# A two-layer diffusion-transformer block on one core: the Exp table load moved to the start of the first scores, pooling bands of 136 columns, and even amounts of other work between layer 2's softmax units

## Chip, core and metric

The kernel runs on one core of a Trainium2 chip. The metric is the device time in microseconds. Each engine (PE for matmuls, DVE and ACT and POOL for the elementwise work, SP for issuing loads) carries out its own list of instructions in order; semaphores make an instruction wait for one of another engine. A difference of 0.2% (3.4 us here) is about what a measurement of this kernel can tell from no change.

## The reference

Two layers of a transformer with 256 image tokens and 256 context tokens, all in float32, batch 1, width 1024. Per layer:

```python
h_x = _half_ffn(h_x, ...); h_c = _half_ffn(h_c, ...)
a_x = _modulate(_rmsnorm(h_x, ...)); p_x = a_x @ w_in[l]
o_a = _neighbourhood_attn(q_a, k_a, v_a, k_a_c, v_a_c, na_rpb[l])   # 4 heads
o_b = _pool_mix(p_x[..., OFF_B_U:OFF_C_Q], pool_w[l], pool_scale[l]) # 4 groups of 64
o_c = _gqa_blocks(q_c, k_all, v_all)                                 # 8 query, 2 key heads
h_x = h_x + mod_x[:, :, 5] * (concatenate([o_a, o_b, o_c]) @ w_out[l])
h_x = _half_ffn(h_x, ...)
```

`_pool_mix` takes, for each of four groups of 64 channels, the mean over a window of 2, 4, 8 or 16 tokens less the token itself, and then a 64x64 product. In layer 1 (of the two) the context tokens go through attention and the second FFN as well; in layer 2 they only give keys and values. The factors `mod` come from `silu(c) @ w_ada`, 38 MB of weights for each layer, which are streamed in.

## The kernel before, in words

Weights come in over SP's queue as float32 blocks of 1 MB (three buffers, `raw`). ACT casts a half of a block to a high part (L309), DVE subtracts to get a low part (L312), and PE does three products for each pair (high-high, high-low, low-high: L351 to L353 in `mm3`). The order of the instructions is fixed when the program is written: `tick` advances a model clock by the estimated time of PE's work, and what was put off with `later` is written out when its time has come. On the chip only the order is left.

The attention part of a layer (`attention`) first makes the keys, the queries and the values of the neighbourhood part. Then `run` goes through the softmax units. Layer 2 has twelve, here u0 to u11; each is two heads for 128 queries: four matmuls for the scores (L1012, L1013), for each head the row maximum on DVE (L1029, with the bias addition L1028 for the first four units), the Exp on ACT (L1037, which also sums), the normalization on DVE (L1040, L1042), and, two units later (`DEPTH`), four transposes on PE for each head (`flip`, L1056) and the copy of the result to SBUF on ACT (L1064). When a pair of heads is complete, `pv` multiplies by the values (L1086) and splits the result (L1090, L1091). Units u4 to u11 need rotated queries, whose split in high and low parts (L892, L893) is `queries`.

Between scores and transposes stands other work for PE, so that the softmax has time: `fill(us)` takes pieces until the model clock has moved on by `us`. The amounts are in the table `FILL`: two numbers for each step of `run`, one list for each layer. The pieces, in this order: the rest of the input products (`rest_in`: four chunks of queries, each evacuated by ACT at L1148 and L1150 and followed by a small matmul for its statistics, L1155; then the values `u` of the pooling), one `pv` that is ready, the pooling (`pooled`), and then the output products of the first 512 inputs (`rest_out`, 96 matmuls in layer 2) in turn with quarters of an `ada` product (`run_ada`, L181, 8 in layer 2, each of which needs a block of 1 MB that has landed). After two chunks `q_post` rotates the queries (L903 on PE, L906 and L910 on DVE, L907 on POOL) and turns the statistics into factors (L392 and on). At the third unit the split of the other part's keys is written (`KEYS_AT`, L881 on ACT, L884 on DVE).

The scores and all these products share five PSUM banks (`mm`), the transposes two (`aux`): a product that is to begin in a bank waits until ACT or DVE has read what was in it.

`pooled` multiplies `u` by a banded matrix of 256x256 for each group. The diagonal blocks of 128x128 come from the tile `pmd` and two corners of 128x8 from `edge`, so that a group takes four matmuls (L1185 to L1187).

ACT's functions come in tables. The Exp table is loaded (ACT_TABLE_LOAD, at L1037) right in front of the first Exp of a layer's attention, and the Silu table again in the next FFN.

Of the kernel before, what the change touches and what calls it, by code (L numbers as in the profile page):

```python
# [9 lines left out]
F32 = mybir.dt.float32  # L10
F32R = mybir.dt.float32r
I32 = mybir.dt.int32
AF = mybir.ActivationFunctionType
# [22 lines left out]
ADA_TOT = (22.0, 22.0, 22.0, 22.0)  # L36
T2K = 12
DEPTH = (2, 2)
FILL = ((3.3, 2.6, 1.8, 2.6, 3.3, 5.5, 0, 0.6, 3.3, 0, 0.6, 1.2, 1.8, 0.6, 4.2, 2.6, 2.6, 0, 0, 0.6, 4.2, 0.6, 1.2, 0, 2.6, 1.2, 0, 1.8, 2.6, 1.2, 2.6, 0, 0.6, 1.2, 0.6, 0.6, 0, 0, 5.5, 2.6), (3.3, 0.6, 2.6, 3.3, 0.6, 3.3, 5.5, 0, 1.8, 1.8, 0.6, 1.8, 0.6, 5.5, 0, 1.2, 1.2, 1.2, 1.2, 1.2, 4.2, 1.2, 0.6, 0.6, 1.8, 0, 2.6, 0.6))
PACE = (0.8, 0.8, 0.8, 0.8, 0.7, 0.8)  # L40
AFTER = ((1.4, 3.5), (1.4, 3.5), (1.4, 3.5), (0.9, 3.0), (1.4, 3.5), (0.9, 4.1))
REFILL = (10.0, 13.0, 13.0, 4.5, 4.5)
# [8 lines left out]
def dit_kernel(  # L51
# [2 lines left out]
    x, c, ctx_in, c_ctx, w_ada, b_ada, norm_g,  # L54
    ffn1_up, ffn1_down, ffn2_up, ffn2_down, w_in, w_out,
    na_rpb, pool_w, pool_scale, q_norm_g, k_norm_g, final_g,
    k_ident, k_rot, k_rope, k_mask, k_pool, k_edge,
    out,
):
    nc = tc.nc  # L60
# [1 line left out]
    const = ctx.enter_context(tc.tile_pool(name="const", bufs=1))  # L62
# [23 lines left out]
    gsc = const.tile([128, 6, KD, 2], F32, name="gsc")  # L86
    hgt = const.tile([128, 4, KD, 2], F32, name="hgt")
    bm = const.tile([128, 2048], F32, name="bm")
    edge = const.tile([128, 2, 4, 8], F32, name="edge")
    pwbd = const.tile([128, 2, 128], F32, name="pwbd")  # L90

    def mm_bank(dt=F32):
# [711 lines left out]
    def attn_prep(l):  # L804

        if l == 0:
            ACT.dma_start(out=mask, in_=k_mask)
            ACT.dma_start(out=rot, in_=k_rot)
            ACT.dma_start(out=edge, in_=k_edge)
            ACT.dma_start(out=rope, in_=k_rope.rearrange("s p t -> p s t"))  # L810
        POOL.memset(bm, NEG)
        POOL.memset(pwbd, 0.0)
        for g in range(4):
            p0 = 64 * (g % 2)
            SP.dma_start(out=pwbd[p0:p0 + 64, g // 2, p0:p0 + 64], in_=pool_w[l, g])


        tab = dramp.tile([4, 64, 465], F32, tag="tab", name="tab")
        SP.dma_start(out=tab, in_=bass.AP(tensor=na_rpb.tensor, offset=l * 4 * 465, ap=[[465, 4], [0, 64], [1, 465]]))

        def go():
            braw = rawp.tile([128, 2048], F32, tag="raw", name="braw")
            bv = braw.rearrange("p (t h k) -> p t h k", t=2, h=4)
            for r in range(4):
                for h in range(4):
                    src = bass.AP(tensor=tab.tensor, offset=tab.offset + h * 64 * 465 + (7 - r) * 31 + 15, ap=[[464, 64], [31, 4], [1, 64]])
                    POOL.dma_start(out=bv[64 * (r % 2):64 * (r % 2) + 64, r // 2, h, :].rearrange("p (a b) -> p a b", a=4), in_=src)
# [14 lines left out]
    def attention(l, a, both):  # L842
# [8 lines left out]
        def carve(n, pat, **kw):  # L851
            r = B[:, o0[0]:o0[0] + n].rearrange(pat, **kw)
            o0[0] += n
            return r
# [3 lines left out]
        kc = carve(512, "p t -> p t")  # L858
        vc = carve(512, "p (b f) -> p b f", b=4)
        vcT = carve(512, "p t -> p t")  # L860
        A = a["t"]
        bmv = bm.rearrange("p (t h k) -> p t h k", t=2, h=4)
        O = [None]
# [113 lines left out]
            pass  # L977


        pmd = [tmp.tile([128, 512], F32, tag="t2k", bufs=T2K, name="pmd") for _ in range(2)]  # L980
        for b in range(2):
            ACT.dma_start(out=pmd[b].rearrange("p (g t) -> p g t", g=4), in_=k_pool[b])


        rq8 = small.tile([128, 40], F32, tag="rq8", bufs=1, name="rq8")
        PT = {}
# [11 lines left out]
        def scores(br, kind, hs, t):  # L998

            if kind == "gqa" and ("na", 0) in K:  # L1000
                for hp in range(2):
                    K.pop(("na", hp))
                st["out"] -= 2
                st["look"] = GQA_LOOK[l]
            S = [mm_bank() for _ in hs]
            q = queries(br, kind, hs)
            kt = K["na", hs[0] // 2] if kind == "na" else K["gqa"]
            keys = slice(0 if br == "x" else TX, NT)
            for tt in ((t,) if br == "x" else (0, 1)):
                for i in range(2):  # L1010
                    o = S[i] if br == "x" else S[i][:, tt * TX:(tt + 1) * TX]
                    PE.matmul(out=o, lhsT=q[:, i, tt * 128:(tt + 1) * 128], rhs=kt[:, i, keys], start=True, stop=False)  # L1012
                    PE.matmul(out=o, lhsT=q[:, i, tt * 128:(tt + 1) * 128], rhs=kt[:, 2 + i, keys], start=False, stop=True)  # L1013
            tick(0.9)
            return [soft(br, kind, h, t, S[i]) for i, h in enumerate(hs)]
# [161 lines left out]
        def pooled(v):  # L1177
            ps = mm_bank()
            pv_ = ps.rearrange("p (c t) -> p c t", c=2)
            for g in range(4):  # L1180
                r0 = 64 * (g % 2)
                o = pv_[r0:r0 + 64, g // 2, :]
                ug = [u[:, 2 * v + tb, g * 64:(g + 1) * 64] for tb in range(2)]
                for tb in range(2):
                    PE.matmul(out=o[:, tb * 128:(tb + 1) * 128], lhsT=ug[tb], rhs=pmd[tb][:, g * 128:(g + 1) * 128], start=(g < 2 and tb == 0), stop=False)  # L1185
                PE.matmul(out=o[:, 128:136], lhsT=ug[0], rhs=edge[:, 0, g, :], start=False, stop=False)
                PE.matmul(out=o[:, 120:128], lhsT=ug[1], rhs=edge[:, 1, g, :], start=False, stop=(g >= 2))  # L1187
            tick(1.7)
            y = tmp.tile([128, 512], F32, tag="t2k", bufs=T2K, name="y")
            ACT.copy(out=y, in_=ps)  # L1190

            def fin():
                ps2 = mm_bank()
                for ch in range(2):
                    PE.matmul(out=ps2[:, ch * TX:(ch + 1) * TX], lhsT=pwbd[:, ch, :], rhs=y[:, ch * TX:(ch + 1) * TX], start=True, stop=True)
                for ch in range(2):
                    s = colsB[:, 104 + 2 * l + ch:105 + 2 * l + ch]
                    oh, ol = acol(O[0], 2 + ch, v * TX, v * TX + TX)
                    ACT.activation(out=oh, in_=ps2[:, ch * TX:(ch + 1) * TX], func=AF.Copy, scale=s)
                    DVE.scalar_tensor_tensor(out=ol, in0=ps2[:, ch * TX:(ch + 1) * TX], scalar=s, in1=oh.bitcast(F32), op0=ALU.mult, op1=ALU.subtract)  # L1200
                missing[0] -= 1
            later(3.0, fin)
# [346 lines left out]
def _constants():  # L1549

    ident = np.eye(128, dtype=np.float32)
    rot = np.zeros((128, 128), np.float32)
    for f in range(128):
        i = f % 32
        if i < 16:
            rot[f + 16, f] = -1.0
        else:
            rot[f - 16, f] = 1.0
    pos = np.arange(256)
    inv = (np.float32(10000.0) ** (-np.arange(0, 32, 2, dtype=np.float32) / np.float32(32))).astype(np.float32)  # L1560
    ar = (pos // 64).astype(np.float32)[:, None] * inv[None]
    ac = (pos % 64).astype(np.float32)[:, None] * inv[None]
    head = np.concatenate([ar, ar, ac, ac], axis=1)
    ang = np.concatenate([head, head], axis=1).T
    rope = np.stack([np.cos(ang), np.sin(ang)]).astype(np.float32)
    col = np.arange(128) % 64
    kcol = np.arange(64)
    w0 = np.clip(col - 8, 0, 48)[:, None]
    mask = ((kcol[None] >= w0) & (kcol[None] < w0 + 16)).astype(np.uint32)
    pool = np.zeros((256, 4, 256), np.float32)  # L1570
    for g, w in enumerate((2, 4, 8, 16)):
        for t in range(256):
            lo, hi = max(t - w // 2, 0), min(t - w // 2 + w, 256)
            pool[lo:hi, g, t] = np.float32(1.0) / np.float32(hi - lo)
            pool[t, g, t] -= np.float32(1.0)
    blocks = np.stack([pool[0:128, :, 0:128], pool[128:256, :, 128:256]])
    edge = np.stack([pool[0:128, :, 128:136], pool[128:256, :, 120:128]], axis=1)
    return {"k_ident": ident, "k_rot": rot, "k_rope": rope, "k_mask": mask, "k_pool": np.ascontiguousarray(blocks), "k_edge": np.ascontiguousarray(edge)}


_INS = ['x', 'c', 'ctx', 'c_ctx', 'w_ada', 'b_ada', 'norm_g', 'ffn1_up', 'ffn1_down', 'ffn2_up', 'ffn2_down',
        'w_in', 'w_out', 'na_rpb', 'pool_w', 'pool_scale', 'q_norm_g', 'k_norm_g', 'final_g']
_CONST = ['k_ident', 'k_rot', 'k_rope', 'k_mask', 'k_pool', 'k_edge']
_OUTS = [((1, 256, 1024), 'float32')]


# [19 lines left out]
```

## Time and profile before

| what | value |
|---|---|
| median of 3 runs | 1686.69 us (1686.47 to 1686.74) |
| the profiled execution | 1686.64 us |
| its span, first to last instruction | 1684.9 us |
| PE busy | 1660.0 us (99%) |
| DVE, ACT, POOL busy | 1055.3, 663.8, 47.8 us |
| granted TensorE clock, mean | 0.998 |
| layer 1's softmax units | from 453.4 us |
| layer 2's softmax units | 1388.8 to about 1472.4 us |

The span is what the profile tells of; 1.7 us of the execution's time lie around it. In the timeline a row has a start, a duration, an engine, a line, an operation with its operands, a count when equal instructions were merged, and in brackets the idle time of the engine before it with what ended it. A matmul's row is longer than its place in the stream: the next one starts before it has drained.

### The profile page before, as it was taken

The page shows a single profiled execution, that of the slowest core. Times are in us where ns is not written, and L with a number is a line of the kernel's source. Part 1 is how long each engine was busy: PE and PEld are TensorE (multiplying, and loading weights), DVE is VectorE, ACT ScalarE, POOL GpSimd, SP SyncE. Part 2 cuts the span into 40 slices and gives each one's busy share as a digit, 9 for nine tenths or more (in the row PEclk, how much of TensorE's full clock was granted, in tenths as well). Part 3 has the DMA queues.
Part 4 walks back from the last instruction along what each step waited for, and adds up shares of the span by engine and source line. Part 5 has one row for each costly group of instructions (what it writes and reads, how often), then busy time and mean ns, then how long its engine had stood idle before and what let it go on. Part 6 is the DMA issues. An engine that isn't in the chain of part 4 may idle for free. (4 is left out here: it accounts for less than half of the span.)

```text
span 1684.9 us, 23252 instructions
## 1 busy us (share of the span) xinstructions
PE 1660.0 (99%) x9256; PEld 1401.6 (83%) x9256; DVE 1055.3 (63%) x1850; ACT 663.8 (39%) x1119; POOL 47.8 (3%) x67
## 2 busy tenths in 40 slices
PE   8999999999999999999999999999999999999997
PEld 5788888889896798888888898888888897799996
DVE  5676567667666776666764476545533567785665
ACT  4332323324556643223233243213232255664543
POOL 0000200000010000000000000020000000010000
PEclk9999999999999999999999999999999999999999
DMA  9755546531305425554553325564533223566551
GB/s 332 206 190 171 161 153 194 167 120 58 113 26 176 132 67 173 166 163 138 175 156 120 87 79 178 161 170 159 155 112 95 81 76 137 202 195 193 179 174 74
DMA packets 284932, 246.97 MB, mean 147 GB/s; under 512 B 9345, under 2 KB 249098, under 8 KB 282776
## 3 DMA queue, kind: packets, MB, share of 16 engines
q1 hardware_dynamic: 281992, 241.30, 46.2%
q0 software_dynamic: 1088, 2.15, 0.6%
q10 hardware_dynamic: 1744, 2.04, 0.4%
q8 instruction: 73, 1.20, 0.3%
q14 instruction: 35, 0.29, 0.1%
HBM read 244.40 MB, written 2.00 MB: 146 GB/s over the span
## 5 line engine op out<-in xcount | busy, mean ns | idle before, releaser
L351 PE MATMUL mm<-act,w 128*128 128x512 f32 (+1 forms) x2016 | 739.1, 367 | 0.0
L352 PE MATMUL mm<-act,w 128*128 128x512 f32 (+1 forms) x2016 | 733.0, 364 | 0.3 <-DVE act L435 0.3
L353 PE MATMUL mm<-act,w 128*128 128x512 f32 (+1 forms) x2016 | 732.9, 364 | 0.0
L312 DVE TENSOR_TENSOR w<-raw,w 128x1024 fp32r<-128x1024 f32 (+1 forms) x307 | 367.6, 1206 | 222.3 <-ACT w L309 221.9
L351 PEld LDWEIGHTS mm<-act,w 128*128 128x128 f32 x2016 | 380.5, 189 | 75.2 <-issue 14.1
L353 PEld LDWEIGHTS mm<-act,w 128*128 128x128 f32 x2016 | 380.4, 189 | 59.7
L352 PEld LDWEIGHTS mm<-act,w 128*128 128x128 f32 x2016 | 380.7, 189 | 59.1 <-DVE act L435 0.5
L309 ACT CAST w<-raw 128x1024 fp32r<-128x1024 f32 (+1 forms) x308 | 313.3, 1031 | 118.8 <-PE mm L353 96.9
L224 DVE SCALAR_TENSOR_TENSOR ada_acc<-ada_raw,sc,ada_acc 128x512 f32<-128x512 f32 x308 | 215.9, 747 | 37.9 <-DMA ada_raw<-in_w_ada_dram 20.9
L562 ACT CAST act<-gf 128x512 fp32r<-128x512 f32 x66 | 40.9, 620 | 269.9 <-DVE gf L559 269.9
L556 ACT ACTIVATE sil<-mm 128x512 f32<-128x512 f32 x66 | 39.3, 596 | 189.4 <-PE mm L353 184.5
L465 DVE SCALAR_TENSOR_TENSOR hT<-mm,hgt,hT 128x256 f32<-128x256 f32 x144 | 63.5, 480 | 76.9 <-PE mm L353 76.6
L559 DVE TENSOR_TENSOR gf<-sil,mm 128x512 f32<-128x512 f32 x65 | 44.7, 687 | 89.5 <-PE mm L353 75.7
L644 PE MATMUL mm<-act,w 128*128 128x258 f32 x352 | 100.2, 285 | 0.0
L645 PE MATMUL mm<-act,w 128*128 128x258 f32 x352 | 99.6, 283 | 0.0
L646 PE MATMUL mm<-act,w 128*128 128x258 f32 x352 | 99.5, 283 | 0.0
L563 DVE TENSOR_TENSOR act<-gf,act 128x512 fp32r<-128x512 f32 x66 | 45.7, 693 | 45.3 <-ACT act L562 45.3
L645 PEld LDWEIGHTS mm<-act,w 128*128 128x128 f32 x352 | 66.8, 190 | 0.3 <-DVE act L618 0.2
L644 PEld LDWEIGHTS mm<-act,w 128*128 128x128 f32 x352 | 66.6, 189 | 0.1
L646 PEld LDWEIGHTS mm<-act,w 128*128 128x128 f32 x352 | 66.4, 189 | 0.0
L377 ACT ACTIVATE sq<-hT 128x256 f32<-128x256 f32 (+1 forms) x45 | 22.5, 500 | 90.8 <-DVE hT L465 90.8
L441 ACT ACTIVATE act<-nt,modT 128x256 fp32r<-128x256 f32 x80 | 39.8, 508 | 37.8 <-DVE nt L440 37.8
(198 smaller groups left out, 1412.1 us busy)
## 6 DMA issues: line engine op xcount, KB each, us to landing
raw<-in_ffn_up_dram SPq DMA_DIRECT2D x170, 512.0 KB
ada_raw<-in_w_ada_dram SPq DMA_DIRECT2D x192, 256.0 KB
raw<-in_ffn_down_dram SPq DMA_DIRECT2D x35, 1024.0 KB
raw<-in_w_ada_dram SPq DMA_DIRECT2D x16, 1024.0 KB
raw<-in_w_in_dram SPq DMA_DIRECT2D x10, 1024.0 KB
raw<-in_ffn_down_dram SPq DMA_DIRECT2D x12, 768.0 KB
raw<-in_w_out_dram SPq DMA_DIRECT2D x8, 1024.0 KB
raw<-in_w_ada_dram SPq DMA_DIRECT2D x12, 512.0 KB
```

The costliest lines, as they stand in the source:

```text
L224: DVE.scalar_tensor_tensor(out=o, in0=raw, scalar=col, in1=o, op0=ALU.mult, op1=ALU.add)
L309: ACT.copy(out=wh, in_=sl)
L312: eng.tensor_tensor(out=wl, in0=sl, in1=wh.bitcast(F32), op=ALU.subtract)
L351: PE.matmul(out=ps, lhsT=wh, rhs=ah, start=start and i == 0, stop=False)
L352: PE.matmul(out=ps, lhsT=wh, rhs=al, start=False, stop=False)
L353: PE.matmul(out=ps, lhsT=wl, rhs=ah, start=False, stop=stop and i == last)
L465: DVE.scalar_tensor_tensor(out=hT[:, k, cols], in0=ps, scalar=gate[:, k, v:v + 1], in1=hT[:, k, cols], op0=ALU.mult, op1=ALU.add)
L559: DVE.tensor_tensor(out=u[:, 0:n], in0=s[:, 0:n], in1=pb[:, 0:n], op=ALU.mult)
L563: DVE.tensor_tensor(out=gl, in0=uv, in1=gh.bitcast(F32), op=ALU.subtract)
L644: PE.matmul(out=ps[:, 0:NX], lhsT=wh, rhs=ah, start=k == 0, stop=False)
L645: PE.matmul(out=ps[:, 0:NX], lhsT=wh, rhs=al, start=False, stop=False)
L646: PE.matmul(out=ps[:, 0:NX], lhsT=wl, rhs=ah, start=False, stop=k == KD - 1)
```

## The change

Three edits.

The Exp table: `scores` now writes, in each layer's first unit, one Exp of a single column (`ones` to `warm`) before the four matmuls, so that the table load stands in front of this one and no longer in front of the first real Exp.

The pooling: the two matrices become one, `bands`, of 136 columns for each half of the tokens, held in free columns of the tile `qkv`; a group takes two matmuls in place of four. The tile `edge` and its load go, and the two `pmd` tiles. The model time of `pooled` is 1.1 in place of 1.7.

The table: layer 2's 28 amounts (0 to 5.5, 48.9 in all) become 28 times 1.7 (47.6 in all). Layer 1's list stays.

```diff
-FILL = ((3.3, 2.6, ...), (3.3, 0.6, 2.6, 3.3, 0.6, 3.3, 5.5, 0, 1.8, 1.8, 0.6, 1.8, 0.6, 5.5, 0, 1.2, 1.2, 1.2, 1.2, 1.2, 4.2, 1.2, 0.6, 0.6, 1.8, 0, 2.6, 0.6))
+FILL = ((3.3, 2.6, ...), (1.7,) * 28)
...
-            ACT.dma_start(out=edge, in_=k_edge)
...
+        bands = carve(1088, "p (b g t) -> p b g t", b=2, g=4)
...
-        pmd = [tmp.tile([128, 512], F32, tag="t2k", bufs=T2K, name="pmd") for _ in range(2)]
         for b in range(2):
-            ACT.dma_start(out=pmd[b].rearrange("p (g t) -> p g t", g=4), in_=k_pool[b])
+            ACT.dma_start(out=bands[:, b], in_=k_pool[b])
...
             q = queries(br, kind, hs)
+            if not PT and not sums:
+
+                warm = small.tile([128, 8], F32, tag="nm", bufs=6, name="nm")
+                ACT.activation(out=warm[:, 0:1], in_=ones, func=AF.Exp)
...
                 ug = [u[:, 2 * v + tb, g * 64:(g + 1) * 64] for tb in range(2)]
-                for tb in range(2):
-                    PE.matmul(out=o[:, tb * 128:(tb + 1) * 128], lhsT=ug[tb], rhs=pmd[tb][:, g * 128:(g + 1) * 128], start=(g < 2 and tb == 0), stop=False)
-                PE.matmul(out=o[:, 128:136], lhsT=ug[0], rhs=edge[:, 0, g, :], start=False, stop=False)
-                PE.matmul(out=o[:, 120:128], lhsT=ug[1], rhs=edge[:, 1, g, :], start=False, stop=(g >= 2))
-            tick(1.7)
+                PE.matmul(out=o[:, 0:136], lhsT=ug[0], rhs=bands[:, 0, g], start=g < 2, stop=False, skip_group_check=True)
+                PE.matmul(out=o[:, 120:256], lhsT=ug[1], rhs=bands[:, 1, g], start=False, stop=g >= 2, skip_group_check=True)
+            tick(1.1)
```

What this does to the order shows best at three places of layer 2. The lines of the changed kernel are off by one or two from those of before (L910 is L909 there, L1029 is L1031, L1056 is L1058).

The first is ACT at the start of the softmax units, before and after. Exp is the ACTIVATE from `mm` to `P,sums`, two for each unit; the pairs that write `qkv` and `qsq` evacuate a chunk of queries; `K` is the split of keys. Before:

```order
L982 DMA pmd<-in_k_pool_dram 128x512 x2
L1037 ACT_TABLE_LOAD
L1037 ACTIVATE P,sums<-mm,nm 128x512 x2
L1148 ACTIVATE qkv<-mm,colsB 128x256
L1150 ACTIVATE qsq<-mm 128x256
L1037 ACTIVATE P,sums<-mm,nm 128x512 x2
L1148 ACTIVATE qkv<-mm,colsB 128x256
L1150 ACTIVATE qsq<-mm 128x256
L881 CAST K<-qkv 64x512 x4
```

The same place on ACT after the change, where L1008 is the new Exp of one column:

```order
L980 DMA qkv<-in_k_pool_dram 128x544 x2
L1008 ACT_TABLE_LOAD
L1008 ACTIVATE nm<-ones 128x1
L1039 ACTIVATE P,sums<-mm,nm 128x512 x4
L1150 ACTIVATE qkv<-mm,colsB 128x256
L1152 ACTIVATE qsq<-mm 128x256
L880 CAST K<-qkv 64x512 x4
L1039 ACTIVATE P,sums<-mm,nm 128x512 x2
L1150 ACTIVATE qkv<-mm,colsB 128x256
L1152 ACTIVATE qsq<-mm 128x256
```

The Exps of u0 and u1 now follow each other, and the second chunk of queries is evacuated behind the key split and the Exps of u2; it stood before the key split.

The second is DVE where the first two chunks of queries are rotated. `rot_t` is the product with the sines, the row that writes `qkv` from it finishes the rotation, and `rs_v` is the first step on the statistics, which reads them from their PSUM bank. Before:

```order
L1040 RECIPROCAL sums<-sums 128x1
L1042 TENSOR_SCALAR P<-P,sums 128x512
L906 TENSOR_TENSOR rot_t<-aux,rope 128x512
L910 TENSOR_TENSOR qkv<-qkv,rot_t 128x2x256
L392 TENSOR_SCALAR rs_v<-mm 128x8
```

The same two steps of the rotation on DVE after the change:

```order
L905 TENSOR_TENSOR rot_t<-aux,rope 128x512
L1030 TENSOR_TENSOR mm<-mm,bm 128x256
L1031 TENSOR_REDUCE nm<-mm 128x1
L1030 TENSOR_TENSOR mm<-mm,bm 128x256
L1031 TENSOR_REDUCE nm<-mm 128x1
L1042 RECIPROCAL sums<-sums 128x1
L1044 TENSOR_SCALAR P<-P,sums 128x512
L1042 RECIPROCAL sums<-sums 128x1
L1044 TENSOR_SCALAR P<-P,sums 128x512
L909 TENSOR_TENSOR qkv<-qkv,rot_t 128x2x256
L391 TENSOR_SCALAR rs_v<-mm 128x8
```

The maxima of u3 and the normalization of u2 now stand between the two steps of the rotation, and the statistics come after them.

The third is PE at the last units: `act,w` is `rest_out`, `ident,P` the transposes, `adasb` those of the ada rows, `PT` the products of values. Before, the last rows:

```order
L352 MATMUL mm<-act,w 128x256
L353 MATMUL mm<-act,w 128x256
L1056 MATMUL aux<-ident,P 128x128 x8
L249 MATMUL aux<-ident,adasb 128x128 x4
L1086 MATMUL mm<-PT,qkv 64x256 x16
```

The last rows of the softmax units on PE after the change, from the second head of u8 on:

```order
L1058 MATMUL aux<-ident,P 128x128 x4
L1014 MATMUL mm<-K,qst 128x512
L1015 MATMUL mm<-K,qst 128x512
L1014 MATMUL mm<-K,qst 128x512
L1015 MATMUL mm<-K,qst 128x512
L1058 MATMUL aux<-ident,P 128x128 x24
L1088 MATMUL mm<-PT,qkv 64x256 x16
```

Before, products of `rest_out` stand between the transposes of the last units; after, the transposes of u9, u10 and u11 (24) follow the last scores with nothing between, since the other work has been written out earlier.

More of the change, by code (lines that the diff above doesn't have):

```diff
@@ L38 @@
 DEPTH = (2, 2)
-FILL = ((3.3, 2.6, 1.8, 2.6, 3.3, 5.5, 0, 0.6, 3.3, 0, 0.6, 1.2, 1.8, 0.6, 4.2, 2.6, 2.6, 0, 0, 0.6, 4.2, 0.6, 1.2, 0, 2.6, 1.2, 0, 1.8, 2.6, 1.2, 2.6, 0, 0.6, 1.2, 0.6, 0.6, 0, 0, 5.5, 2.6), (3.3, 0.6, 2.6, 3.3, 0.6, 3.3, 5.5, 0, 1.8, 1.8, 0.6, 1.8, 0.6, 5.5, 0, 1.2, 1.2, 1.2, 1.2, 1.2, 4.2, 1.2, 0.6, 0.6, 1.8, 0, 2.6, 0.6))
+FILL = ((3.3, 2.6, 1.8, 2.6, 3.3, 5.5, 0, 0.6, 3.3, 0, 0.6, 1.2, 1.8, 0.6, 4.2, 2.6, 2.6, 0, 0, 0.6, 4.2, 0.6, 1.2, 0, 2.6, 1.2, 0, 1.8, 2.6, 1.2, 2.6, 0, 0.6, 1.2, 0.6, 0.6, 0, 0, 5.5, 2.6), (1.7,) * 28)
 PACE = (0.8, 0.8, 0.8, 0.8, 0.7, 0.8)
@@ L56, in dit_kernel @@
     na_rpb, pool_w, pool_scale, q_norm_g, k_norm_g, final_g,
-    k_ident, k_rot, k_rope, k_mask, k_pool, k_edge,
+    k_ident, k_rot, k_rope, k_mask, k_pool,
     out,
@@ L88, in dit_kernel @@
     bm = const.tile([128, 2048], F32, name="bm")
-    edge = const.tile([128, 2, 4, 8], F32, name="edge")
     pwbd = const.tile([128, 2, 128], F32, name="pwbd")
@@ L1575, in _constants @@
             pool[t, g, t] -= np.float32(1.0)
-    blocks = np.stack([pool[0:128, :, 0:128], pool[128:256, :, 128:256]])
-    edge = np.stack([pool[0:128, :, 128:136], pool[128:256, :, 120:128]], axis=1)
-    return {"k_ident": ident, "k_rot": rot, "k_rope": rope, "k_mask": mask, "k_pool": np.ascontiguousarray(blocks), "k_edge": np.ascontiguousarray(edge)}
+    bands = np.stack([pool[0:128, :, 0:136], pool[128:256, :, 120:256]])
+    return {"k_ident": ident, "k_rot": rot, "k_rope": rope, "k_mask": mask, "k_pool": np.ascontiguousarray(bands)}
 _INS = ['x', 'c', 'ctx', 'c_ctx', 'w_ada', 'b_ada', 'norm_g', 'ffn1_up', 'ffn1_down', 'ffn2_up', 'ffn2_down',
         'w_in', 'w_out', 'na_rpb', 'pool_w', 'pool_scale', 'q_norm_g', 'k_norm_g', 'final_g']
-_CONST = ['k_ident', 'k_rot', 'k_rope', 'k_mask', 'k_pool', 'k_edge']
+_CONST = ['k_ident', 'k_rot', 'k_rope', 'k_mask', 'k_pool']
 _OUTS = [((1, 256, 1024), 'float32')]
```

## Prediction

> **What bounds the kernel now.** I read the page first, then who PE waited for, then the timeline of layer 2's softmax units, engine by engine.
>
> ```profile
> PE 1660.0 (99%) x9256; PEld 1401.6 (83%) x9256; DVE 1055.3 (63%) x1850; ACT 663.8 (39%) x1119; POOL 47.8 (3%) x67
> ```
>
> PE is busy for all but 1% of the span, so the end is set by PE's work and by what it waits for. Its waits behind the start, with totals in us, are few:
>
> ```profile
> PE mm L1012 <- ACT P L1037: 1.3, 1, 1.3
> PE aux L1056 <- ACT PT L1064: 1.1, 1, 1.1
> PE ada L181 <- DMA raw<-in_w_ada_dram: 1.0, 1, 1.0
> ...
> PE mm L1155 <- DVE rs_v L392: 0.4, 1, 0.4
> ```
>
> These four are all in layer 2's softmax units, one each: the bank behind the first Exp, a copy of transposes, an ada block, the statistics' bank. With two more of 0.2, at the pooling (its row stands below) and at the last units, they make six and 4.2 us. Layer 1's units show none, so only layer 2 has anything to win. The stretch as a whole (busy us of PE, PEld, DVE, ACT, POOL):
>
> ```profile
> 1388.80:1472.40 83.60, 79.37 (x611) 62.12 (x609) 62.65 (x163) 53.22 (x112) 3.64 (x4) 1.00 0.48 166
> ```
>
> DVE is busy 62.65 of 83.6 us, ACT 53.22: both keep up on average, but three quarters busy and in order, so it matters where their work stands. The old table of amounts left six small waits; the question is how many the even one leaves.
>
> **The change, part by part.** PE's units of time, from the starts of scores (four matmuls, 1388.82 to 1389.75: 0.93) and of products (0.12 from start to start):
>
> ```profile
> 1388.82 0.40 PE L1012 MATMUL mm<-K,qst 128*128 128x512 f32 x1
> ...
> 1389.75 0.28 PE L351 MATMUL mm<-act,w 128*128 128x256 f32 x1
> 1389.87 0.28 PE L352 MATMUL mm<-act,w 128*128 128x256 f32 x1
> ```
>
> *Removed.* The six waits: a row's idle time leaves out the 0.16 us by which a matmul's end (0.28) trails the next start (0.12), so 4.2 + 6 x 0.16 is 5.2 us. I first take all of it off and then add what the new order makes PE wait for, counted from start to start.
>
> *Exp table.* The load lay between maximum and Exp:
>
> ```profile
> 1392.65 0.43 DVE L1028 TENSOR_TENSOR mm<-mm,bm 128x256 f32<-128x256 f32 x1
> 1393.88 1.28 ACT L1037 ACT_TABLE_LOAD   x1 [2.59 <-DVE nm L1029]
> 1395.17 0.69 ACT L1037 ACTIVATE P<-mm,nm 128x512 f32<-128x512 f32 x1
> 1396.00 0.50 PE L1012 MATMUL mm<-K,qst 128*128 128x512 f32 x1 [1.32 <-ACT P L1037]
> ```
>
> ACT had been idle 2.59 us, which covers the load there, and the new Exp of one column; the first real Exp moves from 1395.17 to 1393.88, 1.29 earlier, and frees its bank 0.83 later (1396.00 - 1395.17), at 1394.7. In layer 1 nothing waited for it: 0. The Trainium skill ("ScalarE: Activation LUTs", What ACT_TABLE_LOAD costs) gives about 1283 ns and a drain of about 1380 ns for each switch; the load agrees, but the Exp follows 0.01 us behind the load here, so that no drain stood in this wait. By the page's sum the Exp would move by 2.66 us and my total would be 1.4 lower.
>
> *Pooling.* A group streams 2 x 128 + 2 x 8 columns before and 2 x 136 now, the same 272. Rows:
>
> ```profile
> 1416.67 0.72 PE L1185 MATMUL mm<-pmd,qkv 128*64 128x128 f32 x4 [0.17 <-issue]
> ...
> 1418.99 1.09 PE L1056 MATMUL aux<-ident,P 128*128 128x128 f32 x8
> ```
>
> One pooling takes 2.32 us, 0.58 a group. No row shows 136 columns; between no gain (equal columns, or 0.1 worse a pooling) and a gain of the small matmuls' share, I take 0.2 for each of three poolings, 0.6, nearer to the equal columns. The loads of the bands go into columns free since the keys were written, tens of us ahead: 0; the load of `edge` that goes was hidden.
>
> *Even amounts.* I follow layer 2's new order from 1388.82, with rows' durations. Seven waits and a tail come out.
>
> (A) The order has 18 products, u1's scores and 6 products; then the second chunk needs the bank of u0's first Exp. PE is there at 1389.75 + 24 x 0.12 + 0.93 = 1393.55, the bank comes at 1394.7: 1.15. u2's second head waits 0.2 for u1's first Exp, the first statistics 0.15: 1.5. The preloaded table is thus already spent: by the old order it would have left 0.2.
>
> (B) The second chunk's statistics stand in PE's order behind u2's scores, 36 products, 2 transposed-statistics matmuls and one group of transposes. ACT now evacuates that chunk behind the key split and u2's Exps (the order above). Rows of the same pieces before:
>
> ```profile
> 1399.39 2.52 ACT L881 CAST K<-qkv 64x512 fp32r<-64x512 f32 x4
> ...
> 1405.65 0.46 ACT L1148 ACTIVATE qkv<-mm,colsB 128x256 f32<-128x256 f32 x1
> ```
>
> Between the two stand a unit's maxima and its Exps. From key split to the evacuation's start is 6.26 us, and 0.75 more to its end: 7.0. The split starts when u0's and u1's Exps and the first chunk are off ACT. DVE gives a maximum each 1.07 (0.43 at L1028 above and 0.69 at L1029 in the tail below, which begin a little inside each other), so the fourth Exp starts at 1393.88 + 3 x 1.07 = 1397.1, its chunk's evacuation at 1397.7, the split at 1398.3; the chunk's end is 1405.3. PE is there at 1402.6 (scores end 1397.3; 36 x 0.12; 1.0 for the rest): 2.8.
>
> (C) Third chunk. DVE must finish the rotation and read the old statistics first; that wait was 0.38 before (L1155 in the list), and now the eight rows of u3 and u2 stand ahead of it. The rotation's own pace:
>
> ```profile
> 1412.23 0.69 DVE L906 TENSOR_TENSOR rot_t<-aux,rope 128x512 f32<-128x512 f32 x1 [0.42 <-PE aux L903]
> ```
>
> PE rotates at 1405.75; u3's scores start at 1407.0, its maxima at 1407.7 (0.74 later, see the tail); two of them take 2.15, two normalizations 1.2, the rotation 0.6, `rs_v` 0.3: 1412.0. PE, with scores and 12 products, is there at 1409.35: 2.6.
>
> (D) u4's queries are not split ahead any more (its rotation was late), so they stand behind u1's transposes. Before, without hurry:
>
> ```profile
> 1408.92 1.04 PE L1056 MATMUL aux<-ident,P 128*128 128x128 f32 x8
> ...
> 1410.95 0.85 DVE L893 TENSOR_TENSOR qst<-qkv,qst 64x256 fp32r<-64x256 f32 x2
> ```
>
> From transposes to the first head's low part: 2.45; PE's transposes take 0.88: 1.6.
>
> (E) Three ada quarters now stand in a row behind the pooling. The third block's load is issued when the first output block is split:
>
> ```profile
> 1419.37 2.36 DVE L312 TENSOR_TENSOR w<-raw,w 128x1024 fp32r<-128x1024 f32 x2
> 1422.07 0.80 SPq L157 DMA_DIRECT2D raw<-in_w_ada_dram  x2
> 1426.93 1.06 PE L181 MATMUL ada<-raw,sc 128*32 128x512 f32 x8 [0.99 <-DMA raw<-in_w_ada_dram]
> ```
>
> 4.86 us from issue to PE. After D, u4 starts at 1417.8; 36 products, the rotation and the values of the pooling end at 1424.3; DVE's twelve statistics rows and the split end at 1429.4, the block is there at 1434.6. PE, with one `pv` (16 products of 0.12: 1.9), transposes, scores, pooling and two quarters (1.0 each), is there at 1432.0: 2.5. SP has only these loads behind it.
>
> (F, G, H) Output products wait for `pv`'s split behind u6's Exps (0.7), for the second block's cast and low part behind u7's (2.0: 7.6 us from u4's transposes by the steps of D, a maximum and two Exps, a cast and a low part, 2.25 for both, the low part 1.18 of it by the row at E; PE has 5.6), and the seventh quarter for the buffer this frees (1.0 of its 4.86): 3.7, at most 5, at least 0.
>
> (I) The tail. The 24 transposes have nothing beside them; each pair needs its Exps and a copy to free one of two banks:
>
> ```profile
> 1458.23 0.47 PE L1012 MATMUL mm<-K,qst 128*128 128x512 f32 x1
> ...
> 1458.97 0.69 DVE L1029 TENSOR_REDUCE nm<-mm 128x1 f32<-128x512 f32 x1 [1.82 <-PE mm L1013]
> ...
> 1459.95 0.78 ACT L1037 ACTIVATE P<-mm,nm,rq 128x512 f32<-128x512 f32 x1 [0.80 <-DVE nm L1034]
> ...
> 1461.73 1.07 ACT L1064 COPY PT<-aux 128x512 f32<-128x512 f32 x2
> ```
>
> In this unit of before the maximum starts 0.74 behind the scores and the Exp 0.98 later, and the two Exps take 1.78 until ACT turns to the copies. After the change too ACT turns to u9's copies 3.5 us after u11's scores start, while PE is through scores and u9's transposes in 0.93 + 0.87 + 0.2. One copy (0.55) later u10 may go: 2.0. u11's pair and the `pv` behind it wait 0.3 to 0.4 each for a copy, u8's and u9's copies cost 0.5: 3.3.
>
> *Sum.* 1.5 + 2.8 + 2.6 + 1.6 + 2.5 + 3.7 + 3.3 is 18.0 new, less 5.2 old and 0.6 pooling: +12.2. On the profiled 1686.64 (span and 1.7 around it; 0.05 below the median of 1686.69) that makes 1698.8. Behind the stretch PE is dense, so nothing gives it back.
>
> **Rivals.** (1) The waits for statistics and queries (B, C, D: 7.0) do not come, since they rest on ACT and DVE running as late as I have them; then F to H (3.7) fall away too, PE being early where it was before. Left are A, E, I less old waits and pooling: 7.3 - 5.8 = +1.5, 1688.1, no change. For it: DVE was idle 21 us of the stretch. Against it: the order puts these rows behind each other whatever the pace. It decides at B: if the evacuation is over before 1402.6.
>
> (2) Faster: even amounts do what a spaced pipeline should, PE always finding eight transposes' worth of time, and all old waits go with no new ones: 1686.6 - 5.2 - 0.6 = 1680.8. For it: ACT is 64% busy. Against: the 24 bare transposes, which cannot be hidden. It decides at the tail: less than 1 us lost there and in A to E together.
>
> (3) Slower still: the clock. At the very end the granted clock (third last column) falls once PE stands still, its last matmul ending at 1675.13:
>
> ```profile
> 1675.00:1676.00 1.00, 0.13 (x1) 0.00 (x0) 0.96 (x3) 0.03 (x1) 0.00 (x0) 1.00 0.50 195
> ...
> 1677.00:1678.00 1.00, 0.00 (x0) 0.00 (x0) 0.86 (x2) 0.70 (x2) 0.00 (x0) 0.77 0.00 0
> 1678.00:1679.00 1.00, 0.00 (x0) 0.00 (x0) 0.81 (x5) 0.02 (x1) 0.00 (x0) 0.50 0.00 0
> ```
>
> It fell at about 1677.5, 2.4 us after. B, C and E are that long. If the clock is halved for as long again behind each, PE loses 1.2 us three times: 1702.4. Against it: the 1.3 us wait left it at 1.00. The Trainium skill ("TensorE: Matmul & The Clock Gate", Part 1: The HAM clock gate) has a window of about 3.4 us that runs freely; by it waits of 2.5 to 2.8 us mostly pass, and the end's fall, sooner than 3.4 us, agrees with it only roughly.
>
> **Numbers.** My forecast 0.70, (1) 0.13, (2) 0.06, (3) 0.11. Time 1698.8. My case alone, with F to H from 0 to 5 and a fifth off the others, spans 1692 to 1700; the range takes in (3) and reaches toward (1): 1690.0 to 1702.5, leaving out (2), most of (1). Beyond 0.2% (3.4 us, what a measurement can tell) slower: forecast, (3) and a little of (1), 0.83; within: 0.11; faster: 0.06.
>
> **What would show it.** PE's waits in the new profile: the second chunk's statistics for ACT's square (L1152) about 2.8, the third's for DVE (L391) about 2.6, u4's scores for DVE (L892) about 1.6, an ada quarter for its DMA about 2.5, transposes (L1058) for copies (L1066) at the end about 2 to 3; the first scores no longer for a table load. Layer 1 unchanged within 0.5 us. If layer 2's units, from first scores to the last `pv`, take under 88 us in place of 83.5, I am wrong, and B and C are where I would look first.

## The result, and the profile after

| | before | after |
|---|---|---|
| median of the runs | 1686.58 us (4 runs) | 1700.03 us (4 runs, 1698.61 to 1702.61) |
| ratio, 95% interval | | 1.0081 (1.0068 to 1.0094) |
| profiled execution, span | 1686.64, 1684.9 us | 1698.61, 1696.8 us |
| softmax units of layer 2, in the profile | 83.6 us | 97.0 us |

The forecast was 1698.8 us. PE's waits in the profile after (engine, tile, line, who ended the wait, then the total in us, the times, and the longest), without those of the first 100 us and of the other stages:

```profile
PE ada L180 <- DMA raw<-in_w_ada_dram: 3.3, 2, 2.8
PE mm L1157 <- ACT qsq L1152: 2.5, 1, 2.5
PE mm L1157 <- DVE rs_v L391: 2.4, 1, 2.4
PE aux L1058 <- ACT PT L1066: 2.1, 2, 1.9
...
PE mm L1014 <- DVE qst L892: 1.5, 1, 1.5
PE mm L350 <- ACT P L1039: 1.0, 1, 1.0
...
PE mm L350 <- ACT w L308: 0.9, 1, 0.9
PE mm L352 <- DVE w L311: 0.8, 1, 0.8
```

Six waits of the list before were worth 4.2 us; these are worth 14.5, each at the place where the prediction put it. The profiled execution is the fastest of the four, 1.4 us below their median. DVE and ACT were no busier: over the units (busy us of PE, PEld, DVE, ACT, POOL, then clock, DMA share, GB/s)

```profile
1386.40:1483.40 97.00, 81.97 (x594) 63.12 (x592) 62.55 (x163) 53.54 (x113) 3.64 (x4) 0.98 0.44 147
```

DVE did 62.55 us of work where it had done 62.65, ACT 53.54 for 53.22: the same work in 13.4 us more. It is its place in the queues that changed. One thing more stands in this row, a granted clock of 0.98 where it was 1.00. In finer steps it is one piece:

```profile
1428.00:1430.00 2.00, 1.31 (x16) 0.13 (x4) 1.93 (x6) 0.69 (x2) 0.00 (x0) 1.00 0.88 258
1430.00:1432.00 2.00, 0.00 (x0) 0.00 (x0) 1.13 (x5) 1.45 (x5) 0.00 (x0) 1.00 1.05 352
1432.00:1434.00 2.00, 1.92 (x11) 0.72 (x12) 0.00 (x0) 0.00 (x0) 0.00 (x0) 0.66 0.91 332
1434.00:1436.00 2.00, 2.00 (x7) 1.59 (x6) 0.00 (x0) 0.00 (x0) 0.00 (x0) 0.50 0.97 369
1436.00:1438.00 2.00, 2.00 (x17) 1.17 (x15) 0.68 (x2) 1.18 (x3) 0.00 (x0) 0.98 1.09 422
```

PE stands still for the ada block until 1432.1, and from 1432.65 on it runs at half clock for 3.4 us, which is 1.7 us of its work lost. The other stages moved less. Matmul by matmul against the trace of before, PE is 0.15 us earlier up to layer 1's poolings (508 us), 2.4 earlier behind them and up to layer 2's units, 11.1 later behind these, and 11.1 later at its last matmul; the tail of stores behind that was 0.8 us longer (over the kernels below it was 9.9 to 11.0 us).

So there are three things to test: that the table alone makes the waits, by what stands ahead of what; what the clock adds; and why a pooling, for which 0.2 us was forecast, won more than 1 us in layer 1.

### The profile page after: what moved, and what is told of

It reads as the page before. It is cut to its first block, busy times and chain, and to the rows that moved or that the text cites. A ratio compares the mean times of both kernels' runs of the same rounds, so it can differ in the third digit from the quotient of the medians.

```text
span 1696.8 us, 23156 instructions
## 1 busy us (share of the span) xinstructions
PE 1659.0 (98%) x9208; PEld 1398.8 (82%) x9208; DVE 1055.1 (62%) x1850; ACT 664.7 (39%) x1121; POOL 47.9 (3%) x67
## 3 DMA queue, kind: packets, MB, share of 16 engines
q10 hardware_dynamic: 1600, 2.07, 0.4%
## 4 chain that ended last, share of the span: by engine, by line
PE 91%; DVE 4%; DMA 2%; ACT 2%; issue 1%; SPq 0%; ACTq 0%; DVEq 0%
PE mm L350 24%; PE mm L351 24%; PE mm L352 24%; PE mm L644 3%; PE mm L643 3%; PE mm L645 2%; PE mm L1476 1%; PE mm L1088 1%; DMA raw<-in_w_ada_dram 1%; DVE w L311 1%; PE aux L1058 1%; DMA xin<-in_ffn_up_dram 1%; PE ada L231 1%; DVE nm L1031 1%; PE ada L180 1%
```

## Experiments: the three edits apart

**The table alone.** The kernel before with one line changed:

```diff
-FILL = ((3.3, 2.6, ...), (3.3, 0.6, 2.6, 3.3, ...))
+FILL = ((3.3, 2.6, ...), (1.7,) * 28)
```

> The kernel before with layer 2's amounts alone set to 28 times 1.7. My theory: the whole loss is the table's. Its waits in layer 2's units (17.9 us in the changed kernel's trace) stay, the first one longer by the 1.3 us of the table load, and 5.2 us of old waits go: 1686.6 + 17.9 + 1.3 - 5.2 = 1700.6, and 0 to 4 us more where the granted clock falls behind a wait, so 1700 to 1705. Rival: part of the loss comes from the other two edits (the shorter model time of the pooling, the bands' load on ACT's queue, the new Exp): then this one stays below 1697.

Measured: 1699.08 us (1698.54 to 1701.9), ratio 1.0078 (1.0065 to 1.0091). The rival, that the other two edits carry part of the loss, falls: this one line alone costs 12.6 us, where all three edits together cost 13.5. So with the even table the two small edits won nothing in the time, although layer 1's poolings are 2.3 us shorter with them. My range, 1700 to 1705, began 1 us too high. The longest waits of this kernel:

```profile
PE aux L1056 <- ACT PT L1064: 2.8, 1, 2.8
PE mm L1155 <- DVE rs_v L392: 2.4, 1, 2.4
PE mm L351 <- ACT P L1037: 2.3, 1, 2.3
PE ada L181 <- DMA raw<-in_w_ada_dram: 2.2, 1, 2.2
```

The first Exp's bank costs 1.3 us more than after the change (2.3, 1.0), as worked out for the table load. But the wait for the second chunk's square is nearly gone (0.2 for 2.5). One reason lies in the clock: three of these waits were followed by half a clock, one row of each shown here, while the DMA wait of 2.2 us was not:

```profile
1397.00:1398.00 1.00, 1.00 (x7) 1.00 (x6) 0.80 (x3) 1.00 (x4) 0.00 (x0) 0.50 0.00 0
1414.00:1415.00 1.00, 1.00 (x7) 1.00 (x7) 1.00 (x2) 0.45 (x2) 0.00 (x0) 0.50 0.02 8
1455.00:1457.00 2.00, 1.05 (x10) 0.77 (x6) 1.55 (x2) 0.00 (x0) 0.00 (x0) 1.00 0.98 389
1457.00:1459.00 2.00, 0.77 (x8) 0.16 (x8) 0.00 (x0) 0.00 (x0) 0.00 (x0) 1.00 0.98 352
1479.00:1480.00 1.00, 1.00 (x7) 0.77 (x5) 0.00 (x0) 0.59 (x1) 0.00 (x0) 0.50 0.02 6
```

Counted from the first scores of the units, ACT delivers the square at the same time in both kernels (16.6 us after the change, 16.7 here). PE comes to it 2.4 us later here: 1.3 us of that is the longer first wait, and the other 1.1 us comes with the half clock behind it. So a longer wait or a halved clock is in part paid for by the waits behind it.

**The Exp alone, the bands alone, and both** (the changed kernel with the old amounts). The first is the kernel before with `warm` and its Exp; the second has the bands with their model time; the third is

```diff
-FILL = ((3.3, 2.6, ...), (1.7,) * 28)
+FILL = ((3.3, 2.6, ...), (3.3, 0.6, 2.6, 3.3, ...))
```

> The kernel before with the Exp of one column alone. My theory: the first Exp moves 1.3 us forward, the wait of 1.3 us for its bank falls to 0.2, and what stands behind it (statistics, an ada block) gives part of it back: 1685.4, between 1684.9 and 1686.4. Rival by a drain behind the load as well: 2.6 us earlier, but PE cannot win more than its wait, so the same time, with an Exp more than 1.3 us earlier in the trace. Second rival: the load in front of the first scores' own casts on ACT delays what ACT does there: no gain, 1686.6 or more.

> The kernel before with the pooling's bands alone (and their model time of 1.1). My theory after the changed kernel's trace: a pooling goes from 2.2 us to 1.1 us, three times, 3.4 us off: 1683.2, up to 1 us either way because the shorter model time lets an ada quarter come sooner in layer 2. Rival, the prediction's own term of 0.2 a pooling: 1686.0.

> The changed kernel with layer 2's old amounts put back: the Exp and the bands together. My theory: 3.4 us from the poolings and about 1 us from the Exp: 1682.2, between 1681 and 1684, faster than both kernels. Rival, that the two small edits cost something of their own (about the order or ACT's queue): 1686 or more.

| | us | ratio, 95% interval | expected |
|---|---|---|---|
| Exp alone | 1685.67 | 0.9996 (0.9987 to 1.0004) | 1685.4 |
| bands alone | 1686.28 | 0.9998 (0.9989 to 1.0007) | 1683.2 |
| Exp and bands | 1685.22 | 0.9991 (0.9982 to 1.0000) | 1682.2 |

The Exp does in its trace what was worked out: the first real Exp comes 1.27 us earlier, the wait of 1.3 us for its bank is gone, and PE is 1.0 us ahead behind that place. The table load starts there 0.02 us behind the cast before it, and the small Exp 0.01 us behind the load, so no drain stands there either. In the time it is 0.8 us by the medians, and its interval takes in no change. With the bands my expectation failed. Layer 1's two poolings do give their 2.3 us, and it is lost again in layer 2. PE's longest wait there, in the kernel with both, and the granted clock around it:

```profile
PE aux L1058 <- ACT PT L1066: 2.3, 1, 2.3
```

```profile
1427.00:1430.00 3.00, 0.73 (x4) 0.30 (x4) 2.86 (x9) 2.28 (x6) 0.00 (x0) 1.00 1.02 421
1430.00:1431.00 1.00, 1.00 (x7) 0.93 (x8) 0.97 (x3) 0.85 (x2) 0.00 (x0) 0.66 0.38 148
1431.00:1432.00 1.00, 1.00 (x7) 0.48 (x7) 0.89 (x6) 1.00 (x4) 0.00 (x0) 0.50 0.12 49
...
1433.00:1434.00 1.00, 1.00 (x10) 0.54 (x8) 0.00 (x0) 0.00 (x0) 0.00 (x0) 0.63 0.00 0
```

That wait was 1.1 us before. The shorter model time (1.1) lets one more ada quarter fit behind the pooling; the ones behind it move up as well, and u5 is left with nothing between its scores and the transposes that follow, as u6 had been already, so that PE comes to the transposes behind u6's scores 2.3 us ahead of the copy that they need. The theory for this: not the bands, but the order that their model time makes. It is tested by putting that number back:

```diff
-            tick(1.1)
+            tick(1.7)
```

> The changed kernel with layer 2's old amounts and the pooling's model time back at 1.7: bands and Exp with the instruction order of before. My theory: the run with the old table alone lost its gain because the model time of 1.1 let the ada quarters run ahead and left two units bare, which brought a wait of 2.3 us and a halved clock for about 3 us; with the old order both are gone: 2.3 us from layer 1's poolings, about 1 from layer 2's, 0.9 from the Exp: 1682.5, 1681.8 to 1683.5, and a granted clock of 1.00 through the units. Rival: the wait for the copies grows with any time won ahead of it: 1684.5 or more.

Measured: 1682.73 us (1682.35 to 1683.01), ratio 0.9980 (0.9971 to 0.9989). The two longest waits that are left in the units, where the clock is at 1.00 throughout:

```profile
PE aux L1058 <- ACT PT L1066: 1.1, 1, 1.1
PE ada L180 <- DMA raw<-in_w_ada_dram: 1.0, 1, 1.0
```

So both small edits are good, 3.3 us together (the kernel before had 1686.04 beside this run), as long as the order stays. The two waits that are left can serve each other: an ada quarter in u4 waits for its block, while the transposes two units on have no work ahead of them. Three amounts move the quarter:

```diff
-(..., 5.5, 0, 1.8, 1.8, 0.6, 1.8, 0.6, 5.5, 0, ...)
+(..., 5.5, 0, 1.8, 0.6, 0.6, 0, 0.6, 0, 0, ...)
```

> The kernel of the run with the old order, with three of layer 2's amounts changed (the tenth 0.6, the twelfth and the fourteenth 0), so that the third ada quarter moves from u4 to u5 and the fourth from u5 to u6, where the transposes of the unit had no work ahead of them. My theory: of the two waits left, 1.3 us for the ada block and 1.3 us for a copy of transposes, at most 0.3 each is left: 1682.7 - 2.0 = 1680.7, 1680.2 to 1681.7. Rival: the ada block's quarter only meets its wait later (its buffer comes free later as well), and the next block's: 1682.5.

Measured: 1681.35 us (1680.99 to 1682.27), ratio 0.9970 (0.9958 to 0.9981), and both waits are gone from the list. This kernel beats both.

## Experiments: the waits of the table

**The front.** The changed kernel with the first six amounts as they were.

```diff
-(1.7,) * 28
+(3.3, 0.6, 2.6, 3.3, 0.6, 3.3) + (1.7,) * 22
```

> The changed kernel with the first six of layer 2's amounts as they were (3.3, 0.6, 2.6, 3.3, 0.6, 3.3) and 22 times 1.7 behind them. My theory: the waits at the statistics, the queries and the first Exp come from rows that stand wrongly behind each other, and the order that these six amounts make takes them away: of 8.3 us of front waits about 0.8 are left, the ada block's wait falls from 3.1 to 1 to 2, a wait of about 1.1 for copies comes back, the tail's 3.1 stays: 1700.0 - 9 = 1691, 1689 to 1692.5. Rival: ACT and DVE cannot keep an even pace and the same waits come up a unit or two later: above 1695.

Measured: 1688.5 us (1687.45 to 1689.98), ratio 1.0014 (1.0005 to 1.0023) to before. The rival falls: 11 us go with six numbers, more than I expected (the range began at 1689). In its trace the waits for the square, for u4's queries and for the first Exp's bank are not in the list, and the one for the statistics' bank is 0.5 us:

```profile
PE aux L1058 <- ACT PT L1066: 3.4, 3, 2.2
PE ada L180 <- DMA raw<-in_w_ada_dram: 2.8, 3, 1.6
...
PE mm L1157 <- DVE rs_v L391: 0.5, 1, 0.5
```

So the prediction's A to D come from the order that these six amounts make. What is left is at the copies of transposes (2.2 us of it at the end) and in the ada blocks.

**The tail.** The changed kernel with 16 times 1.7 and 12 times 0.6.

```diff
-(1.7,) * 28
+(1.7,) * 16 + (0.6,) * 12
```

> The changed kernel with the last twelve amounts at 0.6 in place of 1.7, so that work is left for the last transposes; up to u8 the order is the changed kernel's. My theory: the 3.1 us at the bare transposes fall to less than 0.7, and of the 3.4 us for output products and ada blocks about 1 goes too; the front's waits stay: 1700.0 - 2.4 to - 3.9, 1696 to 1697.7. Rival: the engines are late anyway at the end, and the wait only moves to the last product of values: 1699 or more.

Measured: 1696.19 us (1694.78 to 1697.89), ratio 1.0061 (1.0047 to 1.0074) to before: 3.8 us better than the changed kernel by the medians, 3.3 when each is taken against the kernel before of its own series; in the range. No wait for a copy (L1066) is left in the tail. Up to u8 the order is the changed kernel's, yet one wait differs: the square's is 2.5 us in both, the next, for the statistics' bank, 1.5 in place of 2.4. Here the clock was at 0.50 between the two (for 3.4 us from 1404.6), as it was in the kernel with the table alone behind its first wait.

**The key split.** The prediction's B said that the second chunk waits because ACT does the key split first. So the split is written a unit later:

```diff
-KEYS_AT = (2, 2)
+KEYS_AT = (2, 3)
```

> The changed kernel with layer 2's key split written one unit later (at the fourth unit), so that the second chunk's evacuation no longer stands behind it on ACT. My theory: the wait for the square, 2.5 to 2.7 us, falls to 0.5 or less, the wait for the statistics' bank on DVE stays at about 2.5: 1697.8, 1696 to 1698.8 by what the clock does. Rival, that ACT as a whole is too slow there: the 2.5 us of the split come back as a longer wait a unit later (transposes, queries), 1699.5 or more.

Measured: 1701.36 us (1699.49 to 1701.46). The wait for the square is gone, as expected, and all of it is back at the next place. DVE around it, and PE's wait (in brackets the idle time of the engine and what ended it):

```profile
1402.05 0.69 DVE L905 TENSOR_TENSOR rot_t<-aux,rope 128x512 f32<-128x512 f32 x1 [0.28 <-PE aux L902]
1403.63 0.68 DVE L883 TENSOR_TENSOR K<-qkv,K 64x512 fp32r<-64x512 f32 x1 [0.88 <-ACT K L880]
1405.53 0.69 DVE L883 TENSOR_TENSOR K<-qkv,K 64x512 fp32r<-64x512 f32 x1 [1.22 <-ACT K L880]
1406.24 0.43 DVE L1030 TENSOR_TENSOR mm<-mm,bm 128x256 f32<-128x256 f32 x1
...
1409.57 0.69 DVE L909 TENSOR_TENSOR qkv<-qkv,rot_t 128x512 f32<-128x512 f32 x1
1410.17 0.16 DVE L391 TENSOR_SCALAR rs_v<-mm 128x8 f32<-128x8 f32 x1
```

```profile
1410.38 1.02 PE L1157 MATMUL mm<-hind,qsq 128*128 128x2 f32 x4 [5.59 <-DVE rs_v L391]
```

I had moved the split past rows of ACT and forgotten its other half. DVE's two low parts (L883) moved with it, and DVE stands in front of them for ACT's casts, 0.88 and 1.22 us; with their own 1.4 they now stand inside the rotation, ahead of the read that frees the statistics' bank. The wait of 2.4 became 5.6. That is the rival's result, though not by its reason: ACT had itself stood idle for 0.85 us shortly before these casts, so it was not too slow; a row of DVE waited in the wrong place.

## Experiments: what a pooling costs, and what a wait does to the clock

**Poolings.** A pooling of 2.2 us before (three times: 2.19, 2.25, 2.32) took 1.1 to 1.4 with the bands. The columns are the same, 272 a group. In the profile after, in which groups 0 and 1, whose results go to output partitions 0 to 63 and 64 to 127, stand one behind the other in PE's order as L1186, L1187, L1186, L1187, the trace has four rows of L1186 and then four of L1187 (each instruction leaves two rows):

```profile
1426.26 0.46 PE L1186 MATMUL mm<-qkv 128*64 128x136 f32 x4
1426.54 0.41 PE L1187 MATMUL mm<-qkv 128*64 128x136 f32 x4
1426.78 0.45 PE L1186 MATMUL mm<-qkv 128*64 128x136 f32 x4
1427.01 0.45 PE L1187 MATMUL mm<-qkv 128*64 128x136 f32 x4
```

It looks as if the two groups run side by side. Two kernels test it. In the one, the old-order kernel takes its groups in another turn; in the other, the kernel before keeps its four matmuls a group, and writes each for two groups in turn:

```diff
-            for g in range(4):
+            for g in (0, 2, 1, 3):
```

```diff
-            for g in range(4):
+            for g0 in (0, 2):
+                for m in range(4):
+                    for g in (g0, g0 + 1):
...
+                        lo, n = ((0, 128), (128, 128), (128, 8), (120, 8))[m]
```

> The kernel of the run with the old order (bands, Exp, old amounts, model time 1.7), with the four groups of a pooling taken as 0, 2, 1, 3 in place of 0, 1, 2, 3. Groups 0 and 2 write output partitions 0 to 63, 1 and 3 write 64 to 127. My theory: the new pooling costs 1.1 us in place of 2.2 because matmuls for the two halves run side by side when they stand close enough in PE's order; with groups of one half behind each other only the middle pair can: about 1.8 us a pooling, 0.7 more, three times: 1682.7 + 2 = 1684.7. Rival: the gain is of fewer and wider matmuls (136 columns in place of 128 and 8), and the order of groups does nothing: 1.1 us a pooling, 1682.7.

> The kernel before, with its four matmuls a group (128, 128, 8 and 8 columns) written in turn for groups 0 and 1, then 2 and 3. My theory of halves that run side by side: a pooling falls from 2.2 to 1.1 or 1.2 us without any wider matmul, 3 us in all less what waits in layer 2 give back: 1683.5, 1683 to 1685. Rival, that the width of 136 is what pays: 2.2 us as before, 1686.3.

| | a pooling, us (layer 1, 1, 2) | median us | ratio, 95% interval |
|---|---|---|---|
| bands, halves in turn (old order) | 1.08, 1.13, 1.37 | 1682.73 | 0.9980 (0.9971 to 0.9989) |
| bands, halves apart | 1.54, 1.59, 1.65 | 1684.44 | 0.9989 (0.9980 to 0.9998) |
| four matmuls, halves in turn | 1.39, 1.44, 1.52 | 1683.98 | 0.9986 (0.9977 to 0.9994) |
| four matmuls, as before | 2.19, 2.25, 2.32 | 1686.58 | 1 |

The rows of the two (bands apart, then four matmuls in turn), layer 2's pooling:

```profile
1414.71 0.42 PE L1186 MATMUL mm<-qkv 128*64 128x136 f32 x2 [0.17 <-issue]
1414.99 0.45 PE L1187 MATMUL mm<-qkv 128*64 128x136 f32 x2
1415.28 0.45 PE L1186 MATMUL mm<-qkv 128*64 128x136 f32 x4
1415.51 0.45 PE L1187 MATMUL mm<-qkv 128*64 128x136 f32 x4
1415.80 0.40 PE L1186 MATMUL mm<-qkv 128*64 128x136 f32 x2
1416.03 0.40 PE L1187 MATMUL mm<-qkv 128*64 128x136 f32 x2
```

```profile
1415.04 0.73 PE L1188 MATMUL mm<-pmd,qkv 128*64 128x128 f32 x8 [0.17 <-issue]
1415.60 0.35 PE L1188 MATMUL mm<-edge,qkv 128*64 128x8 f32 x8
```

With halves apart the first group stands alone (two rows and two, 0.57 us for one group), the middle two go together (0.52 for both), and the last is alone again. A whole pooling took 1.54 to 1.65 us, where 1.8 was expected. So matmuls for the two halves of the output partitions do run side by side when they are two instructions apart; four apart, as in the kernel before, only the ends of the groups could. Of the 1.0 to 1.1 us that a pooling won, this is at least 0.45 in layer 1 and 0.3 in layer 2 (with halves apart the middle pair still goes together). The four matmuls win 0.8 by the turn alone, less than the 1.0 to 1.1 that I expected, and the bands win 0.15 to 0.3 on top, so the rival holds for that smaller part. The Trainium skill ("TensorEngine Tiling (Array Packing)", Tiling Modes, Key Properties) says that tiles of 64 columns are independent and run matmuls in parallel; these runs agree.

**The clock.** The old-order kernel with sixteen made stalls between 129 and 478 us:

```diff
+    def stall(k):
...
+        PE.transpose(a[:, 0:128], ident, ident)
+        ACT.copy(out=t[:, 0:128], in_=a[:, 0:128])
+        for _ in range(k):
+            POOL.tensor_tensor(out=t[:, 0:128], in0=t[:, 0:128], in1=t[:, 0:128], op=ALU.mult)
...
+        PE.transpose(b[:, 0:128], t[:, 0:128], ident)
```

> The kernel of the run with the old order, with sixteen made stalls of PE of eight lengths in the feed-forward part before layer 1's attention and behind it, 16 us apart: a transpose, a copy on ACT, 1 to 11 products in a row on POOL, and a transpose of the result (this adds work and leaves the output as it is). My theory: the granted clock is halved for 3 to 4 us behind some of the stalls of over 2 us, behind nearly all of over 3.5 us and behind none under 1.5 us, and each such fall costs 1.5 to 2 us beside the stall. Rival: the clock falls for another reason in the softmax units (the mix of work there), and behind these stalls it stays at 1.00.

Measured: 1780.65 us, in one run. Each stall from PE's start to its next start, and the half clock behind its beginning:

| stall, us | halved for |
|---|---|
| 1.16, 2.03 | 0 |
| 2.42, 2.85, 3.19 | 3.41 us each |
| 3.96 to 4.84 (nine) | 3.41 us four times, 6.83 us five times |
| 6.16 | 6.83 us |
| 7.78 | 10.2 us |

The stretch around the stall of 2.42 us, which begins at 244.7 (third last column the clock):

```profile
244.70:247.00 2.30, 0.24 (x2) 0.00 (x0) 1.13 (x2) 0.27 (x1) 1.52 (x3) 1.00 0.00 0
247.00:248.00 1.00, 0.90 (x4) 0.76 (x5) 0.00 (x0) 0.27 (x1) 0.04 (x1) 0.80 0.00 0
248.00:250.00 2.00, 2.00 (x7) 1.51 (x6) 0.11 (x1) 1.31 (x2) 0.00 (x0) 0.50 0.00 0
...
251.00:252.00 1.00, 1.00 (x6) 0.83 (x5) 1.00 (x2) 0.00 (x0) 0.00 (x0) 0.99 0.01 2
```

The theory holds, and more sharply than I had it: every fall lasts a multiple of 3.41 us, and all falls of a run start on one grid of 3.41 us that does not follow the program (those at 152.0, 172.5 and 196.4 us are 6 and 7 steps apart). A window of this grid at full clock in which PE stood for 2.23 us or more, counted from the end of a matmul's place in the stream, was followed by a halved one; 2.07 us in one window was not. A window that is halved already needs less to be followed by another: 1.1 us of standing was enough, 0.4 us was not. This is what parts the nine stalls of like length: five reach at least 1.1 us into a halved window, four end before it begins. The stall of 3.96 us is one of the five; its first halved window, in which PE is busy for 2.31 of 3.41 us, and the next:

```profile
172.52:175.93 3.41, 2.31 (x6) 1.92 (x7) 0.00 (x0) 1.21 (x2) 2.88 (x5) 0.50 0.85 254
175.93:179.35 3.42, 3.42 (x9) 2.65 (x9) 1.37 (x3) 0.00 (x0) 0.00 (x0) 0.50 0.41 105
```

The run is 97.9 us longer than the old order's median, and the stalls themselves are 65.8 us of that. The rest, spread over the 22 halved windows, is at most 1.5 us for each, an estimate from one run.

In the softmax units the line lay between 1.6 and 1.9 us, differently from case to case: 1.7 us in one window of the kernel with work left for the tail was followed by a fall, 1.8 us in one of the changed kernel was not. Why is open. A wait that falls over two windows can pass. The 2.5 and 2.4 us in the changed kernel's profile did, with at most 1.6 us of either in one window, while the 2.8 us for the ada block lay in one window; which of them pass changes with the run. The mean granted clock of its four runs was 0.997, 0.996, 0.995 and 0.993 at 1698.61, 1699.11, 1700.94 and 1702.61 us, and the times rise as the clocks fall. The Trainium skill ("TensorE: Matmul & The Clock Gate", Part 1: The HAM clock gate) has a free-running window of 3413 ns; the traces agree.

## Why the prediction was right, point by point

The time was right, and the mechanism of the waits step by step. That the sums agree to 0.2 us is partly luck: the poolings won 2.8 us more than predicted, and the half clock and the small gaps, which the sum left out, cost 3.4 us. Against the median of the runs, 13.5 us above the kernel before, the forecast is 1.2 us short. Measured from PE's start to its next start, less the matmul's own place in the stream, as the prediction counted:

| step | predicted | in the profile after |
|---|---|---|
| A, bank of the first Exp | 1.5 | 1.4 |
| B, second chunk's statistics (ACT) | 2.8 | 2.7 |
| C, third chunk's statistics (DVE) | 2.6 | 2.5 |
| D, u4's queries | 1.6 | 1.6 |
| E, third ada block | 2.5 | 2.8 |
| F to H, output products, later ada block | 3.7 | 3.1 |
| I, the tail | 3.3 | 3.1 |
| sum of new waits | 18.0 | 17.2 |
| old waits | -5.2 | -5.2 |
| three poolings | -0.6 | -3.4 |
| half clock | 0, and 3.6 as a rival | +1.7 |
| start, end, small gaps (what is left over) | 0 | +1.7 |
| sum | +12.2 | +12.0 |

**Exp table.** Right: "the first real Exp moves [...] 1.29 earlier". It was 1.27. Alone it is worth about 0.8 us by the medians, which the interval does not part from nothing; in the changed kernel it only makes A shorter by 1.3, as the kernel with the table alone shows.

**Even amounts.** A to D and I were read off the order and priced with rows of before; the run with the old front takes A to D away together, and the run with work left for the tail takes I away. E to H came as forecast, but no run takes them away alone. The step from one wait to the next held too: each wait sets when the next engine gets its work, so the chain had to be followed with times, not as a list. B was right in its size, but "behind the key split" told half of it: the split has a DVE part, and moving it moved the wait.

**Poolings.** The term that was mis-sized: "between no gain [...] and a gain of the small matmuls' share, I take 0.2". It was 1.1 to 1.2 for each. I counted columns, which are equal. In the pooling of before the groups stood too far apart to show that two of them run side by side, but another row of before shows it, the products of values, whose two heads go to output partitions 0 to 63 and 64 to 127 in turn:

```profile
1421.94 1.95 PE L1086 MATMUL mm<-PT,qkv 128*64 128x256 f32 x16
```

In the trace the 16 rows start in pairs, 0.01 us apart, one for each half, so that two products of 256 columns take 0.43 us together. By that row four pairs of 136 columns come to an estimated 0.9 us a pooling, near the 1.1 measured.

**Rivals.** The first rival, that the waits B to D do not come, fell: they came. The faster case fell too. The clock came true in part: "If the clock is halved for as long again behind each" was put at three falls, behind B, C and E. The profile has one, behind E; the other runs, by an estimate from their mean clocks, have two to five. It should have been a term of the sum with its own chance for each wait of over 2 us, and not a rival.

## What to carry to other kernels

Even spacing in a planner's model is not even spacing on the chip: amounts that are filled up with whole pieces run ahead (here the work was used up before the transposes of the last three units), and what matters is which row stands in front of the row that frees a bank. Follow each wait through both engines that share a step before moving it. When an operation gets cheaper, keep the order first and change the model's cost second: with the old amounts the bands won 0.2 us alone and 0.5 us beside the Exp, and putting back the old model time brought about 2 us more.

## What was new about the hardware

In these traces a wait of PE has a price step: under about 1.6 us in one 3.41 us window it costs itself, and from about 2.2 us on it brings 3.41 us of half clock, up to 1.7 us of PE's work; between the two it went either way. In a window that is halved already, 1.1 us of standing brought another. And two small float32 matmuls whose outputs lie on different halves of the partitions run side by side if they stand close in PE's order: two instructions apart, two groups took 0.52 us, where one group alone took 0.57.
